# Two modulation vectors move from the first FFN to the first mixer, and the head's banks are emptied into two large buffers

## The chip, the cores and the metric

The kernel runs on one core of one Trainium2 chip. The metric is the device time of that core in microseconds (us). TensorE does the matmuls and the transposes; VectorE, ScalarE and GpSimd do the rest beside it; SyncE's queue issues the loads of the weights. Three runs of the kernel before gave 1095.24, 1098.37 and 1102.44 us, median 1098.37.

## The reference

A decoder trunk of two layers on 256 tokens of width 1024. Each layer is a half-step SwiGLU FFN (width 2816), a mixer with three groups of attention heads behind one input projection, and a second half-step FFN. Each of the three is modulated by nine vectors that come from one condition vector c.

```python
cond = jax.nn.silu(c)
for l in range(DEPTH):
    mod = cond @ ada_w[l] + ada_b[l]          # 1024 x 9216 weights in each layer
    (sh1, sc1, g1, sh2, sc2, g2, sh3, sc3, g3) = jnp.split(mod, N_MOD, axis=-1)
    n1 = modulate(rmsnorm(h, norm_ffn1[l]), sh1, sc1)
    h = h + MACARON_WEIGHT * g1[:, None, :] * swiglu(n1, ffn1_w_gu[l], ffn1_w_down[l])
    n2 = modulate(rmsnorm(h, norm_mix[l]), sh2, sc2)
    h = h + g2[:, None, :] * hybrid_mixer(n2, ...)
    n3 = modulate(rmsnorm(h, norm_ffn2[l]), sh3, sc3)
    h = h + MACARON_WEIGHT * g3[:, None, :] * swiglu(n3, ffn2_w_gu[l], ffn2_w_down[l])
```

The change concerns when sh3 and sc3 of layer 0 are computed: at any time before that layer's second FFN will do.

## The kernel before

**Weights.** All weights are float32 and come in the order of use, mostly as tiles `raw` of 128x2048 (1 MB), of which three exist; `load` (L217) issues each on SyncE's queue. `split` (L235) makes of each half tile a rounded copy `hi` (ScalarE, L243) and the remainder `lo` (VectorE, L244), both 128x1024, and TensorE multiplies hi by hi, hi by lo and lo by hi (L196). So every megabyte of a matmul weight costs VectorE two subtractions and ScalarE two copies.

**Modulation vectors.** A vector's weight is four tiles of 1 MB. `Ada.step` loads one of them and adds its two halves, each times a per-partition value of cond, into `acc` (VectorE, L433 for a vector's first half, L435 for the others): eight VectorE operations in all, and no work for TensorE until `finish`. There a gate (G1, G2, G3) takes a split of `acc`, four matmuls and two copies of ScalarE; a shift or scale (SH, SC) takes eight transposes, two reductions (L460) and one or two small operations. There is one buffer `acc`. ADA_PLAN says which vectors are computed in which sublayer, and `Jobs` spreads their steps, four for each vector, evenly over a number of places: over seven in the first FFN (JOB_PARTS), and in the mixer over the letters j of STEPS.

**Head.** The first FFN has eleven blocks of 256 columns. `lead` computes the first four of them while SC1 and SH1 of layer 0 are still being summed; it uses all eight banks of PSUM (four from psB, four from psA). At its end each bank is emptied by `row_act`: Silu on ScalarE, a multiplication on VectorE (L644), and the product `pr` is transposed back by TensorE (L201) into another bank and copied as a pair chh/chl (L709, L710). Blocks 4 to 10 follow: for each the two halves f of gate and up (`gu_mm`, matmuls into pb, 64 per block), the activation `gu_act` (L717 to L723, with GpSimd), and the products with the down weights (`down`, matmuls into pa, 24 per block) at the places that FIRST_DOWN gives.

**Mixer.** Its work is written as a list of letters in STEPS: M, a, b, q, c, V and p, w are projections that each need weights; h, b and C are heads with their softmax; i and r are the indexer and the eight rounds of the top-k, m the mask that comes of them; v and V are value projections; j is a place of `Jobs`. The scheduler of the tile framework takes the list as the order of emission, with a priority for some parts, and fixes each engine's order when the kernel is built; each engine then works through its own list in order.

Of the kernel before, what the change touches and what calls it, by code (L numbers as in the profile page):

```python
# [10 lines left out]
F32 = mybir.dt.float32  # L11
# [30 lines left out]
FIRST_DOWN = {4: [0, 1], 5: [2], 6: [3, 4], 7: [5], 8: [6, 7], 9: [8, 9], 10: [10]}  # L42
STEPS = [['a0', 'M0', 'M1', 'q1', 'q2', 'i0', 'q4', 'q3', 'q0', 'b1', 'i2', 'b3', 'a1', 'b0', 'j0', 'i4', 'b4', 'a2', 'i6', 'v0', 'r0', 'b2', 'r1', 'v1', 'h2', 'c0', 'c1', 'j1', 'c2', 'r2', 'c3', 'h0', 'j2', 'h4', 'r3', 'r4', 'j3', 'V0', 'V1', 'r5', 'c4', 'r6', 'j4', 'r7', 'm0', 'j5', 'p2', 'j6', 'z0', 'C0', 'p0', 'w0', 'p1', 'w2', 'w1', 'j7', 'p3', 'w3', 'C4', 'p4', 'C2', 'w4'], ['M0', 'M1', 'q4', 'q2', 'q0', 'q1', 'a0', 'i0', 'i2', 'q3', 'b1', 'a1', 'b0', 'i4', 'a2', 'b4', 'i6', 'b3', 'v0', 'r0', 'j0', 'v1', 'b2', 'h0', 'r1', 'c0', 'r2', 'c1', 'h2', 'c2', 'j1', 'j2', 'j3', 'r3', 'c3', 'h4', 'j4', 'j5', 'r4', 'r5', 'r6', 'r7', 'c4', 'V0', 'V1', 'm0', 'C2', 'z0', 'p0', 'p1', 'C0', 'j6', 'p2', 'C4', 'w0', 'p3', 'w2', 'j7', 'p4', 'w3', 'w4', 'w1']]
RS = 0
# [16 lines left out]
NEB = 3  # L61
ADA_PLAN = 'G1.SC2.SH2.SC3.SH3,G2,G3.1SC1.1SH1.1SC2,1SH2.1G1.1SC3.1SH3,1G2,1G3'
NEG = -1e30
# [124 lines left out]
def trunk(ctx, tc, stream, x, cols, rows, positions, rel_bias, ada_b, final_norm, onehot, addc, inv, crow, out, order):  # L188
# [423 lines left out]
    def ffn(l, wgu, wdn, nT, norm_fns, jobs, gate_v, first=False, tail=None):  # L612
# [3 lines left out]
        def get_gu(b):  # L616
            if b not in gu_units_:
                if b and (IO == 2 or IO == 1 and b == 1):
                    r = [load(gu_unit(wgu, l, b, side)) for side in range(2)]
                    w = [split(r[i % 2][:, i // 2 * 1024:(i // 2 + 1) * 1024]) for i in range(4)]  # L620
                    gu_units_[b] = (w[0::2], w[1::2])
                else:
                    gu_units_[b] = tuple(split_unit(load(gu_unit(wgu, l, b, side)), 2048) for side in range(2))
            return gu_units_[b]
# [14 lines left out]

        def row_act(p):  # L640
            sil = three("neg", name=nm("sil"))[:, 0:T]
            S.activation(sil, p[:, 0:256], AF.Silu)
            pr = three("pe", name=nm("pr"))[:, 0:T]
            V.tensor_tensor(pr, sil, p[:, 256:512], op=ALU.mult)  # L644
            return pr

        def lead():
# [25 lines left out]
            for k in range(KD):  # L673
# [20 lines left out]
                if k + 1 < KD:  # L694
                    ws[k + 1] = split_unit(raws[k + 1][2], 2048)
            with tc.high_priority(offset=HP):
                for i in range(LEADB):
                    pr = [row_act(p) for p in banks[i]]
                    p = psB()
                    for f in range(2):  # L700
                        for t in range(NT):
                            PE.transpose(p[:, (2 * f + t) * P:(2 * f + t + 1) * P], pr[t][:, f * P:(f + 1) * P], ident)
                    for f in range(2):
                        if i == LEADB - 1:
                            ch = [wk.tile([P, T], F32R, tag="pT", name=nm("cht"), bufs=PTB) for _ in range(2)]
                        else:
                            ch = chunk_tile()
                        pf = p[:, f * T:(f + 1) * T]
                        S.copy(ch[0], pf)  # L709
                        V.tensor_sub(ch[1], pf, ch[0].bitcast(F32))  # L710
                        act[2 * i + f] = ch

# [28 lines left out]

        def block(b):
            for f in (2 * b, 2 * b + 1):
                p = [psB(), psB()]
                gu_mm(p, f, rows_act if f == 2 else None)
                with tc.high_priority(offset=HP):
                    prior[:] = gu_act(p, f)

        def load_dn(b):
# [12 lines left out]
        if first:  # L762
            lead()
            open_acc()
            for b in range(LEADB, NB):
                now = FIRST_DOWN[b]
                load_dn(now[0])
                get_gu(b)
                if now[0] < NB - SKEW:
                    down_block(now[0])  # L770
                block(b)
                for d in now[1:]:
                    load_dn(d)
# [57 lines left out]
    def mixer(l, nT, norm_fns, jobs):  # L831
# [323 lines left out]
        for s in STEPS[l]:  # L1155
            if s[0] == "w":
                while int(s[1]) not in oT:
                    tick()
            do[s[0]](int(s[1]))
            if s[0] in TICK:  # L1160
                tick()
# [27 lines left out]
    for l in range(DEPTH):  # L1189
        nT, fns = norm(l, SC1, SH1) if l else (pair_tile(), None)  # L1190
        ffn(l, "ffn1_w_gu", "ffn1_w_down", nT, fns, Jobs(plan[l, 1], JOB_PARTS[2 * l]), G1, l == 0)
        nT, fns = norm(l, SC2, SH2)
        mixer(l, nT, fns, Jobs(plan[l, 2], 8))
        nT, fns = norm(l, SC3, SH3)
# [68 lines left out]
```

## Time and profile before

| | |
|---|---|
| median of three runs | 1098.37 us (1095.24 to 1102.44) |
| the profiled execution | 1097.09 us, span 1095.2 us, so 1.9 us lie outside the span |
| TensorE busy in the span | 1049.6 us (96%) |
| VectorE busy | 819.8 us (75%) |
| ScalarE, GpSimd busy | 620.1 us (57%), 194.9 us (18%) |
| mean granted clock of TensorE | 0.991 |

The stages of layer 0, by the timeline of TensorE: `lead` to 64.5 us, the rest of the first FFN ("the head" below) to 234.26, the mixer from there, with the matmuls of its V values (V0, V1) from 323.37, and then the second FFN; after that layer 1. Busy time is a share of the span for each engine; "pb" and "pa" are the two groups of PSUM banks. The granted clock of a stretch is a share of full speed: 1.00 is 2.4 GHz, 0.50 is 1.2 GHz.

### The profile page before, as it was taken

The page shows a single profiled execution, that of the slowest core. Times are in us where ns is not written, and L with a number is a line of the kernel's source. Part 1 is how long each engine was busy: PE and PEld are TensorE (multiplying, and loading weights), DVE is VectorE, ACT ScalarE, POOL GpSimd, SP SyncE. Part 2 cuts the span into 40 slices and gives each one's busy share as a digit, 9 for nine tenths or more (in the row PEclk, how much of TensorE's full clock was granted, in tenths as well). Part 3 has the DMA queues.
Part 4 walks back from the last instruction along what each step waited for, and adds up shares of the span by engine and source line. Part 5 has one row for each costly group of instructions (what it writes and reads, how often), then busy time and mean ns, then how long its engine had stood idle before and what let it go on. Part 6 is the DMA issues. An engine that isn't in the chain of part 4 may idle for free.

```text
span 1095.2 us, 15506 instructions
## 1 busy us (share of the span) xinstructions
PE 1049.6 (96%) x5634; PEld 878.2 (80%) x5634; DVE 819.8 (75%) x1334; ACT 620.1 (57%) x1177; POOL 194.9 (18%) x211
## 2 busy tenths in 40 slices
PE   5999999789999999999999999999999999999997
PEld 3778877668887688888878888887788778888885
DVE  6987877886795787786889877886669757656563
ACT  5554534366666766455555555555676667555561
POOL 1002221122000022232311323131200001222231
PEclk9999999899999999999999999999999999999999
DMA  8978887865355188787848888783536516666541
GB/s 340 373 267 296 293 320 269 334 223 189 111 188 193 64 298 290 270 303 267 293 160 303 292 303 293 281 313 132 188 125 208 178 58 210 233 227 224 212 183 38
DMA packets 38988, 255.84 MB, mean 234 GB/s; under 512 B 4824, under 2 KB 5208, under 8 KB 11008
## 3 DMA queue, kind: packets, MB, share of 16 engines
q1 hardware_dynamic: 38160, 253.14, 63.4%
q0 software_dynamic: 752, 1.71, 0.4%
q8 instruction: 44, 0.72, 0.3%
q14 instruction: 32, 0.26, 0.1%
HBM read 253.76 MB, written 1.07 MB: 233 GB/s over the span
## 4 chain that ended last, share of the span: by engine, by line
PE 80%; issue 6%; DVE 4%; ACT 4%; DMA 3%; POOL 2%; SPq 0%; DVEq 0%; POOLq 0%; ACTq 0%
PE pb L196 41%; PE pa L196 36%; PE pb L201 3%; DMA raw<-in_stream_dram 2%; DVE lo L244 1%; ACT hi L243 1%; DVE up L657 1%; PE pa L201 1%; POOL pr L721 1%; DMA invt<-in_inv_dram 1%; DVE acc L435 1%; POOL chl L723 1%; DMA scr<-gtab 0%; ACT nT L533 0%; ACT z L533 0%
## 5 line engine op out<-in xcount | busy, mean ns | idle before, releaser
L244 DVE TENSOR_TENSOR lo<-raw,hi 128x1024 fp32r<-128x1024 f32 (+3 forms) x314 | 380.7, 1227 | 145.5 <-ACT hi L243 143.5
L243 ACT CAST hi<-raw 128x1024 fp32r<-128x1024 f32 (+3 forms) x314 | 317.7, 1034 | 200.7 <-PE pb L196 94.0
L196 PE MATMUL pb<-nT,hi 128*128 128x512 f32 x1184 | 420.1, 396 | 5.3 <-ACT hi L243 5.3
L196 PE MATMUL pb<-nT,lo 128*128 128x256 f32 x1184 | 333.1, 284 | 2.2 <-DVE lo L244 2.2
L196 PEld LDWEIGHTS pb<-nT,hi 128*128 128x128 f32 x1184 | 222.9, 189 | 56.5 <-ACT hi L243 6.8
L196 PEld LDWEIGHTS pb<-nT,lo 128*128 128x128 f32 x1184 | 224.0, 189 | 6.1 <-DVE lo L244 3.1
L435 DVE SCALAR_TENSOR_TENSOR acc<-raw,cond,acc 128x1024 f32<-128x1024 f32 x118 | 155.5, 1317 | 20.1 <-DMA raw<-in_stream_dram 18.0
L721 POOL TENSOR_TENSOR pr<-sil,pr 128x256 f32<-128x256 f32 x74 | 76.8, 1038 | 516.4 <-DVE pr L718 310.6
L196 PE MATMUL pa<-hi,chh 128*128 128x512 f32 x328 | 105.0, 396 | 0.0
L196 PE MATMUL pa<-lo,chh 128*128 128x512 f32 x328 | 104.6, 392 | 0.4 <-DVE lo L244 0.4
L196 PE MATMUL pa<-hi,chl 128*128 128x512 f32 x328 | 103.3, 393 | 0.0
L196 PE MATMUL pa<-hi,nT 128*128 128x512 f32 (+3 forms) x320 | 89.2, 368 | 2.5 <-ACT nT L561 1.6
L723 POOL TENSOR_TENSOR chl<-pr,chh 128x256 fp32r<-128x256 f32 x74 | 81.7, 1105 | 53.6 <-ACT chh L723 53.6
L196 PEld LDWEIGHTS pa<-lo,chh 128*128 128x128 f32 x328 | 61.6, 189 | 13.5 <-DVE lo L244 0.8
L196 PEld LDWEIGHTS pa<-hi,chl 128*128 128x128 f32 x328 | 61.5, 189 | 13.1 <-issue 0.3
L196 PEld LDWEIGHTS pa<-hi,chh 128*128 128x128 f32 x328 | 60.3, 189 | 13.9 <-ACT chh L723 0.9
L196 PEld LDWEIGHTS pa<-hi,nT 128*128 128x128 f32 x320 | 58.8, 188 | 12.4 <-ACT nT L561 2.2
L196 PE MATMUL pa<-nT,hi 128*128 128x256 f32 x352 | 67.2, 289 | 0.0
L723 ACT CAST chh<-pr 128x256 fp32r<-128x256 f32 x74 | 30.0, 406 | 50.0 <-POOL pr L721 49.6
L196 PE MATMUL pb<-hi,nT 128*128 128x512 f32 x160 | 49.7, 413 | 8.4 <-ACT hi L243 3.9
L196 PEld LDWEIGHTS pa<-nT,hi 128*128 128x128 f32 x352 | 54.7, 189 | 3.3 <-issue 3.1
L196 PE MATMUL pa<-lo,nT 128*128 128x512 f32 (+3 forms) x160 | 54.2, 367 | 0.0
(210 smaller groups left out, 1278.2 us busy)
## 6 DMA issues: line engine op xcount, KB each, us to landing
raw<-in_stream_dram SPq DMA_DIRECT2D x218, 1024.0 KB, 4.9
up<-in_stream_dram SPq DMA_DIRECT2D x16, 512.0 KB, 12.6
raw<-in_stream_dram SPq DMA_DIRECT2D x4, 976.0 KB, 4.7
raw<-in_stream_dram SPq DMA_DIRECT2D x4, 768.0 KB, 4.3
raw<-in_stream_dram SPq DMA_DIRECT2D x4, 640.0 KB, 4.0
brev<-scr POOLq DMA_DIRECT2D x3, 512.0 KB, 10.6
h<-in_x_dram SPq DMA_DIRECT2D x2, 512.0 KB, 4.1
raw<-in_stream_dram SPq DMA_DIRECT2D x2, 512.0 KB, 3.6
```

Of the source, the lines that this page charges most:

```text
L196: last_pe[0] = nc.tensor.matmul(*a, **k)
L201: last_pe[0] = nc.tensor.transpose(*a, **k)
L243: ia = S.copy(hi[:, :n], src)
L244: iv = V.tensor_sub(lo[:, :n], src, hi[:, :n].bitcast(F32))
L435: iv = V.scalar_tensor_tensor(self.acc, src, cond[:, k:k + 1], self.acc, op0=ALU.mult, op1=ALU.add)
L657: V.tensor_tensor_reduce(out=src, in0=src, in1=condb, op0=ALU.mult, op1=ALU.add, scale=scale, scalar=first, accum_out=dst)
L721: G.tensor_tensor(pr, sil, pr, op=ALU.mult)
L723: last = [S.copy(ch[0], pr), G.tensor_tensor(ch[1], pr, ch[0].bitcast(F32), op=ALU.subtract)]
```

## The change

ADA_PLAN moves SC3 and SH3 of layer 0 from the first FFN (which keeps G1, SC2 and SH2, twelve steps over the same seven places) to the mixer, ahead of G2. The mixer's list for layer 0 gets twelve letters j in place of eight; they stand between its start and `r7`, and each is one step, while before four of the eight did one. `Jobs` takes the number of places from the list. In the head all eight banks are first emptied into two tiles `prods` of 128x1024; the transposes become a function `lead_turn`, which is called for the four blocks after the first half (f = 8) of block 4, and the first down weights are loaded behind it. So the weights of block 4 are loaded ahead of those of the first down block, and are split in the order gate, up, gate, up by half tiles.

```diff
--- before.py
+++ after.py
@@ -40,7 +40,7 @@
 LEADB = 4
 JOB_PARTS = [7, 11, 10, 9]
 FIRST_DOWN = {4: [0, 1], 5: [2], 6: [3, 4], 7: [5], 8: [6, 7], 9: [8, 9], 10: [10]}
-STEPS = [['a0', 'M0', 'M1', 'q1', 'q2', 'i0', 'q4', 'q3', 'q0', 'b1', 'i2', 'b3', 'a1', 'b0', 'j0', 'i4', 'b4', 'a2', 'i6', 'v0', 'r0', 'b2', 'r1', 'v1', 'h2', 'c0', 'c1', 'j1', 'c2', 'r2', 'c3', 'h0', 'j2', 'h4', 'r3', 'r4', 'j3', 'V0', 'V1', 'r5', 'c4', 'r6', 'j4', 'r7', 'm0', 'j5', 'p2', 'j6', 'z0', 'C0', 'p0', 'w0', 'p1', 'w2', 'w1', 'j7', 'p3', 'w3', 'C4', 'p4', 'C2', 'w4'], [
...
+STEPS = [['a0', 'M0', 'M1', 'q1', 'q2', 'i0', 'j', 'q4', 'q3', 'q0', 'b1', 'j', 'i2', 'b3', 'a1', 'b0', 'j', 'i4', 'b4', 'a2', 'j', 'i6', 'v0', 'r0', 'j', 'b2', 'r1', 'j', 'v1', 'h2', 'j', 'c0', 'c1', 'j', 'c2', 'r2', 'j', 'c3', 'h0', 'j', 'h4', 'r3', 'j', 'r4', 'V0', 'V1', 'r5', 'c4', 'r6', 'j', 'r7', 'm0', 'p2', 'z0', 'C0', 'p0', 'w0', 'p1', 'w2', 'w1', 'p3', 'w3', 'C4', 'p4', 'C2', 'w4'], [
...
 RS = 0
 SG = 1
 PL = 1
@@ -59,7 +59,7 @@
 TICKS = ['abcvVhC', 'abcvVhCw']
 DN = 0
 NEB = 3
-ADA_PLAN = 'G1.SC2.SH2.SC3.SH3,G2,G3.1SC1.1SH1.1SC2,1SH2.1G1.1SC3.1SH3,1G2,1G3'
+ADA_PLAN = 'G1.SC2.SH2,SC3.SH3.G2,G3.1SC1.1SH1.1SC2,1SH2.1G1.1SC3.1SH3,1G2,1G3'
 NEG = -1e30
 TOPK = T // 4
 IDXH = 8
@@ -615,7 +615,7 @@
 
         def get_gu(b):
             if b not in gu_units_:
-                if b and (IO == 2 or IO == 1 and b == 1):
+                if first and b == LEADB:
                     r = [load(gu_unit(wgu, l, b, side)) for side in range(2)]
                     w = [split(r[i % 2][:, i // 2 * 1024:(i // 2 + 1) * 1024]) for i in range(4)]
                     gu_units_[b] = (w[0::2], w[1::2])
@@ -637,10 +637,11 @@
             passes(p, t, lambda k: (ws[k // 2], slice((k % 2) * 512, (k % 2 + 1) * 512)), nT, between)
             return row_act(p)
 
-        def row_act(p):
+        def row_act(p, pr=None):
             sil = three("neg", name=nm("sil"))[:, 0:T]
             S.activation(sil, p[:, 0:256], AF.Silu)
-            pr = three("pe", name=nm("pr"))[:, 0:T]
+            if pr is None:
+                pr = three("pe", name=nm("pr"))[:, 0:T]
             V.tensor_tensor(pr, sil, p[:, 256:512], op=ALU.mult)
             return pr
 
@@ -693,22 +694,32 @@
                                       start=(k == 0 and x + y == 0), stop=(k == KD - 1 and y == 1))
                 if k + 1 < KD:
                     ws[k + 1] = split_unit(raws[k + 1][2], 2048)
+            prods = [x4(nm("prods")) for _ in range(2)]
+            for f in range(2 * LEADB - 2):
+                act[f] = chunk_tile()
             with tc.high_priority(offset=HP):
                 for i in range(LEADB):
-                    pr = [row_act(p) for p in banks[i]]
-                    p = psB()
-                    for f in range(2):
-                        for t in range(NT):
-                            PE.transpose(p[:, (2 * f + t) * P:(2 * f + t + 1) * P], pr[t][:, f * P:(f + 1) * P], ident)
-                    for f in range(2):
-                        if i == LEADB - 1:
-                            ch = [wk.tile([P, T], F32R, tag="pT", name=nm("cht"), bufs=PTB) for _ in range(2)]
-                        else:
-                            ch = chunk_tile()
-                        pf = p[:, f * T:(f + 1) * T]
-                        S.copy(ch[0], pf)
-                        V.tensor_sub(ch[1], pf, ch[0].bitcast(F32))
-                        act[2 * i + f] = ch
+                    for t, p in enumerate(banks[i]):
+                        c = (i % 2 * NT + t) * T
+                        row_act(p, prods[i // 2][:, c:c + T])
+            return prods
+
+        def lead_turn(prods, i):
+            with tc.high_priority(offset=HP):
+                p = psB()
+                for f in range(2):
+                    for t in range(NT):
+                        c = (i % 2 * NT + t) * T + f * P
+                        PE.transpose(p[:, (2 * f + t) * P:(2 * f + t + 1) * P], prods[i // 2][:, c:c + P], ident)
+                for f in range(2):
+                    if i == LEADB - 1:
+                        ch = [wk.tile([P, T], F32R, tag="pT", name=nm("cht"), bufs=PTB) for _ in range(2)]
+                    else:
+                        ch = act[2 * i + f]
+                    pf = p[:, f * T:(f + 1) * T]
+                    S.copy(ch[0], pf)
+                    V.tensor_sub(ch[1], pf, ch[0].bitcast(F32))
+                    act[2 * i + f] = ch
 
         def gu_act(ps2, f):
             sil = three("neg", name=nm("sil"))[:, 0:T]
@@ -739,12 +750,14 @@
                     S.copy(act[f][0], p[:, 0:T])
                     V.tensor_sub(act[f][1], p[:, 0:T], act[f][0].bitcast(F32))
 
-        def block(b):
+        def block(b, between=None):
             for f in (2 * b, 2 * b + 1):
                 p = [psB(), psB()]
                 gu_mm(p, f, rows_act if f == 2 else None)
                 with tc.high_priority(offset=HP):
                     prior[:] = gu_act(p, f)
+                if between:
+                    between(f % 2)
 
         def load_dn(b):
             dn_units_[b] = split_unit(load(dn_unit(wdn, l, b)), 2048, b >= NB - 2)
@@ -760,15 +773,26 @@
                     down(f, t, range(2))
 
         if first:
-            lead()
+            prods = lead()
+            get_gu(LEADB)
             open_acc()
+
+            def between(i):
+                if i == 0:
+                    for j in range(LEADB):
+                        lead_turn(prods, j)
+                    load_dn(0)
+
+            block(LEADB, between)
             for b in range(LEADB, NB):
                 now = FIRST_DOWN[b]
-                load_dn(now[0])
-                get_gu(b)
+                if b > LEADB:
+                    load_dn(now[0])
+                    get_gu(b)
                 if now[0] < NB - SKEW:
                     down_block(now[0])
-                block(b)
+                if b > LEADB:
+                    block(b)
                 for d in now[1:]:
                     load_dn(d)
                     if d < NB - SKEW:
@@ -1156,7 +1180,7 @@
             if s[0] == "w":
                 while int(s[1]) not in oT:
                     tick()
-            do[s[0]](int(s[1]))
+            do[s[0]](int(s[1:] or 0))
             if s[0] in TICK:
                 tick()
         while pend:
@@ -1190,7 +1214,7 @@
         nT, fns = norm(l, SC1, SH1) if l else (pair_tile(), None)
         ffn(l, "ffn1_w_gu", "ffn1_w_down", nT, fns, Jobs(plan[l, 1], JOB_PARTS[2 * l]), G1, l == 0)
         nT, fns = norm(l, SC2, SH2)
-        mixer(l, nT, fns, Jobs(plan[l, 2], 8))
+        mixer(l, nT, fns, Jobs(plan[l, 2], sum(x[0] == 'j' for x in STEPS[l])))
         nT, fns = norm(l, SC3, SH3)
         ffn(l, "ffn2_w_gu", "ffn2_w_down", nT, fns, Jobs(plan[l, 3], JOB_PARTS[2 * l + 1]), G3, tail=load_final if l == DEPTH - 1 else None)
     for t in range(NT):
```

Three places show what moves. First TensorE at the end of `lead`. Before, the transposes of the products pr follow the last matmul of lead (into pa_183), and the first down matmuls (into pa_594) stand between them:

```order
L196 MATMUL pa_183<-lo_477,nT_107 128x512
L201 MATMUL pb_518<-ident,pr_512 128x128
L201 MATMUL pb_518<-ident,pr_516 128x128
...
L201 MATMUL pb_539<-ident,pr_533 128x128
L201 MATMUL pb_539<-ident,pr_537 128x128
...
L201 MATMUL pb_560<-ident,pr_554 128x128
L196 MATMUL pa_594<-hi_600,chh_523 128x512
L196 MATMUL pa_594<-lo_601,chh_523 128x512
L196 MATMUL pa_594<-hi_600,chl_524 128x512
L201 MATMUL pb_560<-ident,pr_558 128x128
```

After, pb_572 and pb_573 are the two banks of the first half of block 4, and the four groups of transposes, of the products in `prods`, stand in and behind its matmuls; pa_568 is the first down product:

```order
L196 MATMUL pb_573<-nT_107,lo_557 128x256
L201 MATMUL pb_618<-ident,prods_510 128x128 x4
L196 MATMUL pb_573<-nT_107,hi_556 128x512
...
L196 MATMUL pb_573<-nT_107,lo_557 128x256
L201 MATMUL pb_627<-ident,prods_510 128x128 x4
L201 MATMUL pb_636<-ident,prods_511 128x128 x4
L201 MATMUL pb_645<-ident,prods_511 128x128 x4
L196 MATMUL pa_568<-hi_660,chh_512 128x512
```

The first of the transposes stands in place of row 197 at row 219, behind 22 more matmuls, and the down products come behind all sixteen.

Second, VectorE at the start of the mixer, where each of the remainders `lo` frees a half tile of weights. Before (ta, tb and cc are the rotation of a part of the queries, rep a copy of it):

```order
L826 TENSOR_TENSOR ta_2107<-cc_2095,cosf 128x64
L827 TENSOR_TENSOR tb_2108<-cc_2095,sinf 128x2x16
L828 TENSOR_TENSOR tb_2108<-cc_2095,sinf 128x2x16
L829 TENSOR_TENSOR cc_2095<-ta_2107,tb_2108 128x2x32
L888 COPY rep_2113<-cc_2095 128x128
L244 TENSOR_TENSOR lo_2174<-raw_2171,hi_2173 128x1024
L244 TENSOR_TENSOR lo_2178<-raw_2171,hi_2177 128x1024
L244 TENSOR_TENSOR lo_2288<-raw_2285,hi_2287 128x1024
L244 TENSOR_TENSOR lo_2292<-raw_2285,hi_2291 128x1024
```

After, the first two accumulations of SC3 (acc_2337) stand ahead of the same splits:

```order
L433 TENSOR_SCALAR acc_2337<-raw_2338,cond 128x1024
L850 TENSOR_TENSOR ta_2038<-cc_2026,cosf 128x64
L851 TENSOR_TENSOR tb_2039<-cc_2026,sinf 128x2x16
L852 TENSOR_TENSOR tb_2039<-cc_2026,sinf 128x2x16
L435 SCALAR_TENSOR_TENSOR acc_2337<-raw_2338,cond,acc_2337 128x1024
L853 TENSOR_TENSOR cc_2026<-ta_2038,tb_2039 128x2x32
L244 TENSOR_TENSOR lo_2105<-raw_2102,hi_2104 128x1024
L244 TENSOR_TENSOR lo_2109<-raw_2102,hi_2108 128x1024
L912 COPY rep_2044<-cc_2026 128x128
L244 TENSOR_TENSOR lo_2219<-raw_2216,hi_2218 128x1024
L244 TENSOR_TENSOR lo_2223<-raw_2216,hi_2222 128x1024
```

Such accumulations, with their loads on SyncE's queue, then stand between the splits of all the projections up to the V values.

Third, VectorE at the end of the top-k. Before, the V weights' last remainder (lo_3057) stands ahead of the last rounds of the top-k and of the mask msk:

```order
L938 MAX m_635_3193<-work_2279 128x8 x2
L244 TENSOR_TENSOR lo_3057<-raw_3050,hi_3056 128x640
L939 MATCH_REPLACE work_2279<-m_635_3193,work_2279 128x128
L939 MATCH_REPLACE work_2279<-m_635_3193,work_2279 128x256
L435 SCALAR_TENSOR_TENSOR acc_2889<-raw_3204,cond,acc_2889 128x1024
L938 MAX m_636_3198<-work_2279 128x8 x2
L435 SCALAR_TENSOR_TENSOR acc_2889<-raw_3204,cond,acc_2889 128x1024
L939 MATCH_REPLACE work_2279<-m_636_3198,work_2279 128x128
L939 MATCH_REPLACE work_2279<-m_636_3198,work_2279 128x256
L244 TENSOR_TENSOR lo_3154<-raw_3151,hi_3153 128x1024
L942 TENSOR_SCALAR msk_2280<-work_2279 128x384
```

After, the mask stands ahead of the V weights' first remainder (lo_3041), and accumulations of G2 (acc_2934) between the remainders:

```order
L966 TENSOR_SCALAR msk_2211<-work_2210 128x384
L1064 RECIPROCAL sm_2975<-sm_2975 128x2
L1055 ISA neg_3014,sm_3015<-pb_2999,biasm 128x128
...
L244 TENSOR_TENSOR lo_3041<-raw_3038,hi_3040 128x640
L435 SCALAR_TENSOR_TENSOR acc_2934<-raw_3029,cond,acc_2934 128x1024
L244 TENSOR_TENSOR lo_3045<-raw_3038,hi_3044 128x640
L1070 TENSOR_SCALAR pe_2978<-pe_2978,sm_2975 128x256
L1064 RECIPROCAL sm_2985<-sm_2985 128x2
```

Here the four splits of the V weights moved from ahead of the last two rounds of the top-k to behind the mask and behind four more softmax pieces (ISA, negation and sum). From the end of the mixer on, the orders of all engines are the same as before.

## Rows read from the trace of the kernel before

**Rows 1.** Page, the chain that ended last: shares of the span by engine.

```profile
PE 80%; issue 6%; DVE 4%; ACT 4%; DMA 3%; POOL 2%; SPq 0%; DVEq 0%; POOLq 0%; ACTq 0%
```

**Rows 2.** Stretches: length, busy PE, PEld, DVE, ACT, POOL, PEclk, DMA share, GB/s.

```profile
64.50:233.60 169.10, 154.78 (x766) 127.86 (x765) 138.53 (x176) 78.80 (x132) 34.44 (x37) 0.95 0.79 289
...
233.60:321.20 87.60, 85.91 (x556) 72.93 (x555) 70.55 (x194) 57.56 (x141) 6.81 (x13) 1.00 0.46 160
...
300.00:325.00 25.00, 25.00 (x186) 22.43 (x185) 23.78 (x85) 16.07 (x41) 0.00 (x0) 1.00 0.57 198
400.00:550.00 150.00, 150.00 (x802) 129.19 (x801) 116.44 (x127) 80.32 (x130) 43.38 (x37) 1.00 0.80 290
25.00:50.00 25.00, 24.25 (x103) 19.03 (x103) 24.52 (x37) 13.82 (x20) 0.00 (x0) 1.00 1.00 404
```

**Rows 3.** TensorE's waits from 64 to 234 us: total, times, longest.

```profile
PE pb L196 <- ACT hi L243: 5.3, 3, 2.7
PE pb L201 <- DVE pr L644: 2.5, 1, 2.5
PE pa L196 <- POOL chl L723: 2.3, 3, 1.3
PE pb L196 <- DVE lo L244: 2.2, 2, 1.5
```

**Rows 4.** Shorter stretches, columns as in Rows 2.

```profile
150.00:233.60 83.60, 71.79 (x343) 57.98 (x342) 66.28 (x78) 39.17 (x63) 17.29 (x19) 0.92 0.78 291
...
205.00:210.00 5.00, 2.48 (x7) 1.78 (x8) 4.40 (x4) 2.40 (x3) 0.00 (x0) 0.50 0.84 308
...
270.00:275.00 5.00, 4.88 (x29) 3.00 (x28) 1.23 (x1) 2.78 (x7) 2.99 (x8) 1.00 0.50 198
```

**Rows 5.** TensorE's timeline: start, length, operation, [idle before <- releaser].

```profile
67.73 0.85 PE L201 MATMUL pb<-ident,pr 128*128 128x128 f32 x4 [2.51 <-DVE pr L644]
...
74.43 0.39 PE L196 MATMUL pb<-nT,hi 128*128 128x512 f32 x1
...
234.26 1.06 PE L201 MATMUL pb<-ident,z 128*128 128x128 f32 x8
```

**Rows 6.** The chain in layer 0's second FFN: start, length, what.

```profile
439.87 11.19 PE pb L196 x64
451.06 5.47 PE pa L196 x24
```

**Rows 7.** VectorE's groups from 64.5 to 233.6: count, busy us, mean ns, idle.

```profile
L435 DVE SCALAR_TENSOR_TENSOR acc<-raw,cond,acc 128x1024 f32<-128x1024 f32 x36 | 47.2, 1311 | 2.1 <-DMA raw<-in_stream_dram 1.7
...
L460 DVE TENSOR_REDUCE modc<-pb 128x4 f32<-128x512 f32 x8 | 5.2, 685 | 2.9 <-PE pb L201 2.8
...
L433 DVE TENSOR_SCALAR acc<-raw,cond 128x1024 f32<-128x1024 f32 x4 | 3.0, 744 | 0.0
```

**Rows 8.** VectorE's groups from 233.6 to 321.2, columns as in Rows 7.

```profile
L244 DVE TENSOR_TENSOR lo<-raw,hi 128x1024 fp32r<-128x1024 f32 x15 | 18.1, 1221 | 2.9 <-ACT hi L243 2.8
L435 DVE SCALAR_TENSOR_TENSOR acc<-raw,cond,acc 128x1024 f32<-128x1024 f32 x6 | 7.8, 1298 | 5.5 <-DMA raw<-in_stream_dram 5.4
L244 DVE TENSOR_TENSOR lo<-raw,hi 128x768 fp32r<-128x768 f32 x4 | 3.8, 959 | 5.0 <-ACT hi L243 5.0
...
L244 DVE TENSOR_TENSOR lo<-raw,hi 128x640 fp32r<-128x640 f32 x4 | 3.3, 814 | 0.0
...
L1031 DVE CUSTOM_DVE_ANT_0 neg<-pb,biasm 128x256 f32<-128x256 f32 x7 | 2.9, 420 | 0.0
```

**Rows 9.** VectorE's timeline in the mixer, columns as in Rows 5.

```profile
273.77 2.70 DVE L435 SCALAR_TENSOR_TENSOR acc<-raw,cond,acc 128x1024 f32<-128x1024 f32 x2 [5.07 <-DMA raw<-in_stream_dram]
...
320.85 0.36 DVE L942 TENSOR_SCALAR msk<-work 128x384 fp32r<-128x384 f32 x1
```

**Rows 10.** TensorE's timeline in the mixer, first V matmul and first with the mask.

```profile
323.37 0.41 PE L196 MATMUL pa<-hi,nT 128*128 128x320 f32 x1
...
337.50 0.44 PE L196 MATMUL pb<-msk,identr 128*128 128x128 f32 x2
```

More of the change, by code (lines that the diff above doesn't have):

```diff
@@ L42 @@
 FIRST_DOWN = {4: [0, 1], 5: [2], 6: [3, 4], 7: [5], 8: [6, 7], 9: [8, 9], 10: [10]}
-STEPS = [['a0', 'M0', 'M1', 'q1', 'q2', 'i0', 'q4', 'q3', 'q0', 'b1', 'i2', 'b3', 'a1', 'b0', 'j0', 'i4', 'b4', 'a2', 'i6', 'v0', 'r0', 'b2', 'r1', 'v1', 'h2', 'c0', 'c1', 'j1', 'c2', 'r2', 'c3', 'h0', 'j2', 'h4', 'r3', 'r4', 'j3', 'V0', 'V1', 'r5', 'c4', 'r6', 'j4', 'r7', 'm0', 'j5', 'p2', 'j6', 'z0', 'C0', 'p0', 'w0', 'p1', 'w2', 'w1', 'j7', 'p3', 'w3', 'C4', 'p4', 'C2', 'w4'], ['M0', 'M1', 'q4', 'q2', 'q0', 'q1', 'a0', 'i0', 'i2', 'q3', 'b1', 'a1', 'b0', 'i4', 'a2', 'b4', 'i6', 'b3', 'v0', 'r0', 'j0', 'v1', 'b2', 'h0', 'r1', 'c0', 'r2', 'c1', 'h2', 'c2', 'j1', 'j2', 'j3', 'r3', 'c3', 'h4', 'j4', 'j5', 'r4', 'r5', 'r6', 'r7', 'c4', 'V0', 'V1', 'm0', 'C2', 'z0', 'p0', 'p1', 'C0', 'j6', 'p2', 'C4', 'w0', 'p3', 'w2', 'j7', 'p4', 'w3', 'w4', 'w1']]
+STEPS = [['a0', 'M0', 'M1', 'q1', 'q2', 'i0', 'j', 'q4', 'q3', 'q0', 'b1', 'j', 'i2', 'b3', 'a1', 'b0', 'j', 'i4', 'b4', 'a2', 'j', 'i6', 'v0', 'r0', 'j', 'b2', 'r1', 'j', 'v1', 'h2', 'j', 'c0', 'c1', 'j', 'c2', 'r2', 'j', 'c3', 'h0', 'j', 'h4', 'r3', 'j', 'r4', 'V0', 'V1', 'r5', 'c4', 'r6', 'j', 'r7', 'm0', 'p2', 'z0', 'C0', 'p0', 'w0', 'p1', 'w2', 'w1', 'p3', 'w3', 'C4', 'p4', 'C2', 'w4'], ['M0', 'M1', 'q4', 'q2', 'q0', 'q1', 'a0', 'i0', 'i2', 'q3', 'b1', 'a1', 'b0', 'i4', 'a2', 'b4', 'i6', 'b3', 'v0', 'r0', 'j0', 'v1', 'b2', 'h0', 'r1', 'c0', 'r2', 'c1', 'h2', 'c2', 'j1', 'j2', 'j3', 'r3', 'c3', 'h4', 'j4', 'j5', 'r4', 'r5', 'r6', 'r7', 'c4', 'V0', 'V1', 'm0', 'C2', 'z0', 'p0', 'p1', 'C0', 'j6', 'p2', 'C4', 'w0', 'p3', 'w2', 'j7', 'p4', 'w3', 'w4', 'w1']]
 RS = 0
```

## The prediction, made before the changed kernel ran

> **What bounds the kernel.** I read the chain of waits first: 80% of the span is TensorE's own work [rows 1]. Time is won or lost only where TensorE stands still or runs below full clock, or where its work changes; here its matmuls stay the same. So I looked for such stretches with the windows [rows 2]. Before `lead` ends the change alters nothing. From 64.5 to 233.6 us TensorE is busy 154.78 of 169.10 us, at a mean granted clock of 0.95. In the mixer up to 321.2 it is busy 85.91 of 87.60 at 1.00, and VectorE only 70.55 (81%). The second FFN, with the same blocks as the head, shows no idle time at all: 150.00 of 150, with VectorE at 116.44 (78%) and the loads at 290 GB/s. The head runs VectorE at 138.53 of 169.10 (82%) and does lose time; it has five modulation vectors to sum where the second FFN has four.
>
> What the head loses, I worked out from blocks at full pace: 11.19 us for a block of gate and up, 5.47 for one of down [rows 6]. Seven and eleven of them are 78.3 + 60.2 = 138.5 us; the 16 transposes of lead's products, the four vectors' 32 and the gate's few matmuls come to about 7.2 at 1.06 for eight transposes [rows 5]. That is 145.7 us of work in the 169.8 from 64.5 to the mixer's first transpose at 234.26 [rows 5]: **24.1 us lost**. Of it 14.3 (169.10 - 154.78 [rows 2]) are idle and the rest is slow clock: from 205 to 210, behind idle time, the clock was 0.50, which is 1.2 GHz, and TensorE busy 2.48 of 5 [rows 4]. So a microsecond of idle here costs 24.1 / 14.3 = 1.7 us.
>
> Where it is lost: 2.51 of the idle time are one wait at lead's end, for a product pr that VectorE makes [rows 3, 5]; up to 74.43, where block 4 begins [rows 5], TensorE does 13 transposes and 18 down matmuls, some 5.8 us of work in 9.9, so 4.1 are lost there. The other 20.0 lie behind 150 us, where 83.60 - 71.79 = 11.8 are idle [rows 4], for a weight's hi or lo (7.5 in both) and for the down inputs [rows 3].
>
> **The change part by part.** (a) *Two vectors fewer in the head.* Eight loads of 1 MB go, and on VectorE 2 x 0.744 + 14 x 1.311 = 19.8 us of sums and 4 x 0.685 = 2.7 of reductions [rows 7], about 23 with the small ones. TensorE's 16 transposes (2.1 us) go to the mixer with them: no gain. VectorE is left with 115.5 us for some 154, 75%, under the 78% at which the second FFN has no wait; the loads come to (289 x 169.1 - 8390) / 154, about 263 GB/s, under its 290. If that holds everywhere, the 11.8 us of idle vanish. The bounds are 0 and 11.8 us left. I take 2, nearest to the row of the second FFN, since the head still has three vectors in seven lumps and its first split waits for ScalarE; 2 x 1.7 = 3.4 us lost.
>
> (b) *The emptying at lead's end.* The wait of 2.51 goes: TensorE has 22 matmuls of block 4 to do, 3.9 us at 11.19 / 64, before and among the first transposes. What is late next: the fourth group of transposes needs a bank of block 4's first half, and VectorE's addition that frees it stands behind a subtraction of 1.22 [rows 8]; I estimate 2.1 us of idle. Then the first down matmul needs its weight and input from ScalarE, behind block 4's own copies: another 1.3. 3.4 x 1.7 = 5.8 us, where 4.1 are lost now. Bounds: nothing, when both are ready, and 10, when VectorE also has an accumulation ahead. So this part alone costs 1.7 us.
>
> The head gains 24.1 - 3.4 - 5.8 = **15 us** (bounds 24 and 0).
>
> (c) *Twelve steps in the mixer.* All come before r7, with their 8.4 MB in the same queue as the weights. The memory has room: 160 GB/s now [rows 2], 14.0 MB; 22.4 MB in about 92 us are 243, under 290. TensorE's 2.1 us were counted as moved. VectorE is the question, since each of its sums stands in one list with the remainders lo that TensorE needs. The mixer's first matmul that all this precedes is that of the V weights. VectorE's work before it: 70.55 now, less 7.8 for six sums and 26.4 for all splits (one more of 1.2 beside those of [rows 8]), leaves 36.4. Add the splits that now stand ahead of it, 14 x 1.221 + 4 x 0.959 + 0.814 + 1.2 = 22.9 [rows 8]; the sums, 18 x 1.298 + 2 x 0.744 = 24.9 [rows 7, 8]; four reductions, 2.7; and some 3.5 of small ones and four softmax pieces that were behind it. That is **90.4 us**. TensorE reaches the V matmul 323.37 - 233.6 = 89.8 us after the start [rows 10], with the 2.1 of transposes and about 0.9 of another head 92.8. VectorE must be busy 97% of that time for no stall. It was 98% from 25 to 50 us and 95% from 300 to 325, with TensorE 25.00 of 25 busy there [rows 2]; over the mixer it is 81%, but there it has no more work. I take 95%, the row of the same kind of work: 95.2 us, 2.4 late. The V weights' next remainders have two sums of 1.30 between them where none were: I add 1.3. At 1.7, that is **6 us** lost (bounds 0, at 98%, and 35, at 81%).
>
> (d) *The mask* came at 320.85 and was wanted at 337.50 [rows 9, 10]: 16 us of cover, and it moves ahead of the V weights, so nothing. If it were more than 16 us late, everything behind it would be too. G2 is wanted only with the mixer's last output, behind all the heads. The second FFN's norm finds SC3 and SH3 done long before; nothing else of it changes.
>
> Sum: -15 + 6 = **-9 us** on the profiled execution's 1097.09, which is 1.28 under the median of the runs shown. On the median's scale 1098.37 - 9 = **1089**.
>
> **One rule against it.** At 273.77 VectorE stood 5.07 us for the load of a sum [rows 9], and TensorE was busy 4.88 of the 5 us from 270 to 275 [rows 4]: one such wait was covered. The Trainium skill (TensorE: Matmul & The Clock Gate, the section Architectural detail: the array is 16× 32×32, not 1× 128×128) says that ACT and DVE queues are strict FIFO, so a sum whose load is late holds every remainder queued behind it. The trace agrees in that VectorE did nothing else in those 5 us, not in a price for TensorE. By the rule the sum would be that of the rival D below, by the row of TensorE that of (c); both are worked out from rows alone.
>
> **The rivals.** *B: both halves better.* The head becomes like the second FFN (nothing left of 2 us idle), and VectorE keeps 97% in the mixer. -24.1 + 5.8 + 1, about -17: 1081. For it: the 78% row. Against: the list of the mixer is twice as dense with sums as any that the trace shows over 90 us. *C: the head is only half cured.* Idle time behind 150 us waits for hi of ScalarE too (5.3 of it [rows 3]), which is not overloaded, so the loads' arrival in the three raw buffers may be what is late. Then half of 20.0 stays, the head gains 10 - 1.7 = 8, and the mixer takes 6 to 10: -2 to +2, so 1096 to 1100. *D: slower.* VectorE's list in the mixer waits again and again for the loads of sums, as at 273.77, and its share stays near 81%. 90.4 / 0.805 = 112.3, which is 19.5 behind TensorE's 92.8, and with the 1.3, at 1.7, costs 35: -15 + 35 = +20, 1118. It decides from the share at which the loss equals the head's 15: 15 / 1.7 - 1.3 = 7.5 late, 90.4 / 100.3 = 90%. Against it: in the densest stretch, 300 to 325, VectorE had 95%, and at 81% it had nothing to do for part of the time. *That the change does nothing* is excluded by the order of the instructions.
>
> **The numbers.** 1% is 11 us, about what a measurement of this kernel can tell from no change; faster means under 1087.4, slower over 1109.4. The forecast (1084 to 1095) has 0.45, of which 0.17 is faster; B 0.22, all faster; C 0.21, all the same; D 0.12, of which 0.02 comes out the same at a share near 88%. Faster 0.17 + 0.22 = 0.39, with 0.01 of C's lucky end 0.40; slower 0.10 and 0.01 for a late mask, 0.11; same 0.49. The range from 1079 (B with a little more) to 1103 (C's upper end and a bit) leaves out D and the ends of B, some 0.15 to 0.2. B, the forecast and C have one sign or none; D alone the other.
>
> **What would show it.** Right: from 75 us to the mixer TensorE waits 4 us or less and at a clock of 1.00; the mixer's first transpose comes at about 219, not 234; at lead's end the 2.51 is gone and two waits of one to two us appear, for VectorE's sil and for ScalarE's chh; the first V matmul comes about 95 us behind the mixer's start, with a wait for lo of 2 to 4 us ahead. Wrong: waits for hi of over 6 us in the head (C), or a V matmul over 100 us behind the mixer's start with VectorE idle for raw (D).

## The result, and the profile after

The changed kernel took 1104.26 us (median of 14 runs, 1099.53 to 1112.75), the kernel before 1097.19 (14 runs). The ratio is 1.0071, 95% interval 1.0047 to 1.0096: **slower by 0.7%**, where 1089 was forecast and the range ended at 1103. The profiled execution has a span of 1104.3 us, 9.1 more than before.

The windows of the changed kernel, columns as in [rows 2], show the head in two pieces, then the mixer up to its first V matmul, the V matmuls themselves, and the whole mixer:

```profile
64.50:80.00 15.50, 11.57 (x56) 9.55 (x56) 12.11 (x20) 7.80 (x19) 2.35 (x2) 0.80 0.79 305
80.00:219.97 139.97, 136.82 (x694) 113.93 (x692) 105.38 (x134) 69.80 (x113) 36.46 (x33) 1.00 0.72 262
219.97:325.20 105.23, 93.81 (x589) 78.91 (x589) 85.68 (x220) 56.54 (x143) 13.35 (x15) 0.96 0.52 188
325.20:335.00 9.80, 8.01 (x32) 6.89 (x33) 8.76 (x22) 6.37 (x18) 0.00 (x0) 0.58 0.63 221
219.97:381.61 161.64, 147.16 (x858) 119.72 (x859) 122.88 (x299) 91.61 (x226) 15.78 (x18) 0.95 0.52 188
```

The same two stretches of the mixer before, up to the first V matmul and from there to the next norm:

```profile
234.26:323.37 89.11, 87.49 (x569) 74.39 (x570) 71.01 (x197) 58.74 (x143) 6.81 (x13) 1.00 0.47 166
323.37:373.38 50.01, 48.75 (x275) 38.12 (x274) 31.64 (x80) 32.86 (x84) 2.56 (x3) 1.00 0.40 147
```

TensorE's timeline of the changed kernel, columns as in [rows 5], has the two waits at lead's end, the mixer's first transpose, the first two V matmuls, and the next norm's transposes:

```profile
73.14 0.66 PE L201 MATMUL pb<-ident,prods 128*128 128x128 f32 x4 [2.10 <-DVE pr L729]
75.63 1.22 PE L196 MATMUL pa<-hi,chh 128*128 128x512 f32 x2 [1.83 <-ACT chh L720]
...
219.97 1.06 PE L201 MATMUL pb<-ident,z 128*128 128x128 f32 x8
...
325.20 0.63 PE L196 MATMUL pa<-hi,nT 128*128 128x320 f32 x1 [4.92 <-ACT hi L243]
327.27 0.63 PE L196 MATMUL pa<-lo,nT 128*128 128x320 f32 x1 [1.44 <-DVE lo L244]
...
381.61 1.06 PE L201 MATMUL pb<-ident,z 128*128 128x128 f32 x8 [0.46 <-DVE z L511]
```

Three differences add up. The mixer began 14.3 us earlier (219.97, before 234.26 [rows 5]). It lasted 161.64 us, before 139.12: 22.5 longer. Behind it another 0.9 were lost. -14.3 + 22.5 + 0.9 = 9.1. The head gained most of what was forecast, and the mixer gave it all back and more. Of the 22.5, 16.1 lie ahead of the first V matmul (105.23 against 89.11) and 6.4 behind it, where the clock granted in the V matmuls was 0.58 of full speed, near the level of 1.2 GHz. Over the whole mixer TensorE was idle 14.5 us (161.64 - 147.16), before 2.9, so 11.6 of the 22.5 are idle time. Another 2.1 are the 16 transposes that moved, and the remaining 8.8 are the mixer's own work at a lower clock: the granted clock was 0.95, before 1.00.

TensorE's waits of the changed kernel, in the head and then in the mixer (total, times, longest):

```profile
PE pb L201 <- DVE pr L729: 2.1, 1, 2.1
PE pa L196 <- ACT chh L720: 1.8, 1, 1.8
PE pa L196 <- ACT chh L734: 1.1, 2, 0.7
PE pb L196 <- DVE lo L244: 1.0, 1, 1.0
PE pb L196 <- ACT hi L243: 0.8, 1, 0.8
```

```profile
PE pa L196 <- ACT hi L243: 4.9, 1, 4.9
PE pa L201 <- ACT pe L1068: 2.6, 1, 2.6
PE pb L201 <- POOL iqq L853: 1.8, 1, 1.8
PE pa L196 <- DVE lo L244: 1.8, 2, 1.4
```

The head's waits for hi and lo fell from 7.5 us [rows 3] to 1.8. In the mixer there are four new lines of over 1.5 us, where no line was over 0.8 us before; one of three such lines of before is:

```profile
PE pa L196 <- ACT nT L561: 0.8, 1, 0.8
```

**The longest of them, followed back.** The chain of waits of the changed kernel around the V matmuls (start, length, what):

```profile
312.01 0.97 POOL acc L426
312.98 0.28 issue
313.26 2.54 DMA acc<-in_ada_b_dram
315.81 0.26 DVE work L963
316.07 1.09 issue
317.16 1.29 DVE acc L435
318.44 0.40 DVE work L963 x2
318.84 0.07 DVE chl L1103
318.91 0.18 issue
319.09 1.28 DVE acc L435
320.37 0.03 DVE m L962
320.39 4.01 DMA raw<-in_stream_dram
```

The last row is the load of the V weights. It could be issued only at 320.39, when a sum of G2 (319.09) had freed a raw tile. That sum had waited for the memset of the one buffer acc (312.01) and the load of G2's bias into it (313.26), and the memset for SH3's transposes. So the V weights, which need nothing of G2, were late by way of the shared raw tiles and the one acc. The delay of the sums began earlier, as VectorE's and TensorE's timelines show:

```profile
258.16 1.37 DVE L435 SCALAR_TENSOR_TENSOR acc<-raw,cond,acc 128x1024 f32<-128x1024 f32 x1
...
286.44 0.42 DVE L1103 TENSOR_TENSOR chl<-pb,chh 128x256 fp32r<-128x256 f32 x1 [5.03 <-ACT chh L1103]
286.78 1.28 DVE L460 TENSOR_REDUCE modc<-pb 128x4 f32<-128x512 f32 x2
287.98 0.74 DVE L433 TENSOR_SCALAR acc<-raw,cond 128x1024 f32<-128x1024 f32 x1
```

```profile
285.92 1.09 PE L201 MATMUL pb<-ident,acc 128*128 128x128 f32 x8
```

SC3's last sum was done by 259.5, but its transposes stand at 285.92 in TensorE's list, so SH3's first sum came at 287.98. In between VectorE stood waiting for TensorE's and ScalarE's results; it was idle for 19.6 us (105.23 - 85.68) in the mixer up to the V matmul, and its longest waits there were:

```profile
DVE work L956 <- ACT rel L953: 6.0, 3, 3.8
DVE chl L1103 <- ACT chh L1103: 5.0, 1, 5.0
DVE lo L244 <- ACT hi L243: 2.8, 2, 1.9
...
DVE acc L433 <- DMA raw<-in_stream_dram: 0.6, 1, 0.6
```

For a sum's load it waited 0.6 us, not 5.07 at a time as at 273.77 before [rows 9]. In this stretch the sums hardly waited for loads, and the one load followed here, that of the V weights, waited for a sum.

### The profile page after: what moved, and what is told of

It reads as the page before. It is cut to its first block, busy times and chain, and to the rows that moved or that the text cites. A ratio compares the mean times of both kernels' runs of the same rounds, so it can differ in the third digit from the quotient of the medians.

```text
span 1104.3 us, 15493 instructions
## 1 busy us (share of the span) xinstructions
PE 1054.6 (96%) x5634; PEld 881.2 (80%) x5634; DVE 819.0 (74%) x1334; ACT 616.9 (56%) x1177; POOL 207.6 (19%) x211
## 4 chain that ended last, share of the span: by engine, by line
PE 76%; issue 7%; DMA 5%; DVE 5%; ACT 4%; POOL 2%; SPq 0%; DVEq 0%; POOLq 0%; ACTq 0%
PE pb L196 40%; PE pa L196 34%; DMA raw<-in_stream_dram 4%; PE pb L201 2%; DVE lo L244 2%; ACT hi L243 1%; DVE up L658 1%; DVE acc L435 1%; DMA invt<-in_inv_dram 1%; POOL pr L732 1%; PE pa L201 0%; ACT z L533 0%; POOL chl L734 0%; ACT nT L533 0%; ACT nT L561 0%
## 5 line engine op out<-in xcount | busy, mean ns | idle before, releaser
L732 POOL TENSOR_TENSOR pr<-sil,pr 128x256 f32<-128x256 f32 x74 | 84.8, 1146 | 498.5 <-DVE pr L729 374.7
L196 PEld LDWEIGHTS pa<-lo,chh 128*128 128x128 f32 x328 | 61.9, 189 | 13.1
```

Of the source, the lines that this page charges most:

```text
L196: last_pe[0] = nc.tensor.matmul(*a, **k)
L732: G.tensor_tensor(pr, sil, pr, op=ALU.mult)
```

## The experiments

Two theories were set first. Theory L: the V weights' load is held in the raw tiles, as the chain shows. Theory W: VectorE has too much work ahead of the V weights. "Head" below is the time of the mixer's first transpose, "mixer" the time from it to the next norm's.

**One part alone.** The kernel before with the new ADA_PLAN and the new list of STEPS, and the changed kernel with the old ones:

```diff
-ADA_PLAN = 'G1.SC2.SH2.SC3.SH3,G2,...'
+ADA_PLAN = 'G1.SC2.SH2,SC3.SH3.G2,...'
-        mixer(l, nT, fns, Jobs(plan[l, 2], 8))
+        mixer(l, nT, fns, Jobs(plan[l, 2], sum(x[0] == "j" for x in STEPS[l])))
```

> Only the move of SC3 and SH3 to the mixer with its twelve places; lead's end is the old one. Theory L (loads held: in the mixer the three raw buffers hold tiles whose sums VectorE's list puts late, so the V weights' load is issued late): the mixer's first transpose at 216 to 219 us (15 to 18 earlier than 234.26), the mixer about 22 us longer than before, the V matmuls again behind a wait for hi of 4 to 6 us; 1099 to 1104 us. Theory W (VectorE has too much work ahead of the V weights): the same times. Rival E (the emptying at lead's end is what costs): as fast as the head's gain, 1080 to 1084 us.

> Only the rewrite of lead's end; plan and places are the old ones. Theories L and W: 1098 to 1102 us, 1 to 4 us more than before, all of it between 64 and 85 us (two waits of about 2 us and half clock behind them). Rival E: 1104 us or more.

The plan alone: 1105.00 us, ratio 1.0058 (1.0043 to 1.0073), head 215.98, mixer 166.2. Lead's end alone: 1098.20, ratio 0.9997 (0.9986 to 1.0008), head 236.03 (1.8 later than before), mixer 139.1. So rival E falls: the moved vectors make the loss, and lead's new end costs nothing that can be told from its runs' times. The plan alone began the mixer 4.0 us earlier than the changed kernel, but its mixer lasted 4.5 longer, and the medians of the two kernels are 0.7 apart, within their spread.

**The V weights' load set free.** The twelve loads go to pairs of large tiles instead of raw tiles:

```diff
-            raw = load(ada_unit(l, v, i))
+            raw = load_halves(ada_unit(l, v, i)) if (l, v) in OWN else load(ada_unit(l, v, i))
```

> The changed kernel, but the twelve loads for SC3, SH3 and G2 of the first mixer go to pairs of 128x1024 tiles of the pool of large buffers instead of raw tiles; same bytes, same sums. Theory L: the V weights' load is no longer behind a sum; first V matmul 92 to 96 us behind the mixer's first transpose (105.2 in the changed kernel) with a wait of at most 1 us; 1086 to 1092 us. Theory W: VectorE still has the same 25 us of sums among the splits; the V matmul 102 us or later behind the start, or the same stall at another place of the mixer; 1099 to 1104 us.

1116.39 us, ratio 1.0156 (1.0133 to 1.0179). The wait at the V matmul was gone and it came 101.4 us behind the start, but the mixer lasted 172.1 us, with these waits of TensorE ahead:

```profile
PE pa L201 <- ACT pe L1079: 11.6, 6, 4.4
PE pa L201 <- DVE pe L1081: 3.8, 3, 2.3
```

The stall moved to the softmax pieces. **Theory L as the whole cause falls**, with a reserve: the edit also moved the sums in VectorE's list, and in this order VectorE did wait for the sums' loads, by its waits in the mixer:

```profile
DVE acc L446 <- DMA ada<-in_stream_dram: 7.0, 7, 1.8
DVE acc L444 <- DMA ada<-in_stream_dram: 6.9, 1, 6.9
```

**Half of the sums left out.** The loads stay, of each only the first half is summed:

```diff
-            for kk in range(2):
+            for kk in range(1 if (l, v) in ((0, SC3), (0, SH3), (0, G2)) else 2):
```

> The changed kernel with the second half of each of the twelve loads not summed (left out: half of SC3, SH3 and G2's sums); loads, transposes and places stay. Theory W: about 13 us less for VectorE ahead of the V weights; no wait there, the first V matmul 93 us behind the mixer's first transpose; 1087 to 1091 us. Theory L: SH3's first sum still waits for SC3's transposes (at 286 in the changed kernel) and the V weights' load still for a sum that stands behind the top-k; only the sums left out behind 287 us (8 x 1.3 = 10 us of VectorE) come off, the V matmul 97 to 101 us behind the start, still with a wait of 2 us or more; 1094 to 1099 us.

1094.10 us, ratio 0.9965 (0.9949 to 0.9980); no wait for hi, V matmul 94.6 us behind the start, but mixer 150.1. The V matmul is near theory W's place, the total is theory L's: with 13.5 us less of VectorE's work the mixer was 11.6 shorter, and it was still 11 longer than before. (With fewer sums the scheduler also built a somewhat different order for VectorE.)

**Other places.** A new theory P: only the places were wrong. The places of the twelve steps were moved; the list shows the letters behind which a j stands (SC3, SH3, G2):

```
early:          a0 M1 i0 q0 | b1 i2 b3 b0 | v1 c0 c2 c3
G2 late:        i0 b1 b0 a2 | r0 r1 h2 c1 | r6 m0 p2 w1
early, G2 late: a0 M1 i0 q0 | b1 b3 b0 b4 | r6 m0 p2 w1
SC3 only:       i0 b1 b0 a2 |             | r6 m0 p2 w1   (SH3 stays in the first FFN)
```

> The changed kernel with its twelve places earlier: SC3's four behind a0, M1, i0, q0, SH3's behind b1, i2, b3, b0, G2's behind v1, c0, c2, c3; loads, sums and transposes are the same, all twelve still ahead of the V weights. Theory P (the places, not the sum of the work: in the changed kernel VectorE stands idle for 20 us from 259 to 287 because SC3's transposes, and with them the one buffer of the sums and the raw tiles, come 27 us behind its last sum, and is full from 287 to 326): SC3's transposes come by 265 us, VectorE is idle for under 10 us from 255 to 290, the first V matmul 95 to 98 us behind the mixer's first transpose (105.2 in the changed kernel), 1088 to 1093 us. Theory W (VectorE has too much work ahead of the V weights, wherever it stands): V matmul 102 us behind or later, 1099 to 1106 us.

> The changed kernel with G2's four places moved behind the V weights (r6, m0, p2, w1); SC3 and SH3 stay where they are. Theory W: 9 us of sums less ahead of the V weights, V matmul 94 to 96 us behind the mixer's first transpose, and VectorE has room behind it: 1088 to 1092 us. Theory P: the V load is free of G2's sums, but SH3's still bunch behind SC3's late transposes: V matmul 96 to 99 us behind, the waits near 300 us stay; 1092 to 1097 us.

> SC3's and SH3's places early (behind a0, M1, i0, q0, b1, b3, b0, b4) and G2's behind the V weights. Theories P and W: no wait over 1.5 us in the mixer, V matmul 92 to 94 us behind its first transpose, the head's 14 us kept but for the 2 us of transposes: 1083 to 1088 us. If it is not under 1090, neither the places nor the work ahead of the V weights is what holds the mixer.

> SH3 stays in the first FFN (sixteen steps over seven places); only SC3 goes to the mixer, at the first four of the changed kernel's places, G2 behind the V weights as in the run before. Theory W: mixer 141 to 143 us long; the head keeps part of its loss (mixer's first transpose at 224 to 230): 1088 to 1095 us. Theory P says the same of the mixer; it is a measure of the head with four vectors.

Early: 1100.92 us, ratio 1.0035 (1.0017 to 1.0052). SC3's transposes came at 259.84 and VectorE was busier ahead of the V weights than in any other run with twelve steps there, and still the V matmul came 106.7 us behind the start: **theory P falls** on its main number, and both of theory W's hold (102 us or later, 1099 to 1106). Its window up to the V matmul:

```profile
218.04:324.78 106.74, 93.57 (x581) 78.85 (x581) 92.67 (x217) 58.61 (x143) 10.26 (x17) 0.94 0.62 226
```

G2 late: 1097.77, ratio 1.0007 (0.9994 to 1.0020), V matmul 98.9 behind, mixer 153.2 (the profiled execution, 1094.11, was the shortest of the ten). Taking G2's four steps from ahead of the V weights took away the wait for hi and 6.3 us ahead of them. The run does not part the price of the chain shown above from that of G2's sums, since both left that stretch. The V matmul is where theory P had it; the total missed both expectations, theory P's by 0.8.

Early and G2 late: 1094.29, ratio 0.9965 (0.9947 to 0.9983), faster than both kernels, but over the 1090 set as a bound: its V matmul came 97.9 us behind, its mixer lasted 151.0. By that bound neither the places nor the work ahead of the V weights is the whole of it. Its windows, to the V matmul and from there:

```profile
219.23:317.12 97.89, 91.79 (x585) 77.55 (x586) 86.86 (x217) 57.39 (x143) 8.81 (x15) 0.98 0.59 212
317.12:370.21 53.09, 50.22 (x274) 39.21 (x274) 35.04 (x83) 33.32 (x84) 2.45 (x3) 0.97 0.51 185
```

SC3 only: 1104.81, ratio 1.0061 (1.0046 to 1.0076). Expected were a head of 224 to 230 and a mixer of 141 to 143; measured 233.29 and 146.2. By the reckoning of the prediction a head with four vectors loses 168.8 - 144.6 = 24.2 us. With the same new end of lead, one with five loses 171.5 - 145.7 = 25.8 (from the run with lead's end alone), and one with three 11.9. Nearly the whole gain of the head comes with the second vector.

**Work and loads by themselves.** Two new theories, V (VectorE's time) and R (the loads). First the sums cut to 32 of 1024 columns (all but SC3's and SH3's first) with all loads kept; then the sums kept with three loads instead of twelve, in the kernel with own tiles, where the order of VectorE and TensorE stays the same:

```diff
+                    n = 32 if (l, v) in ((0, SC3), (0, SH3), (0, G2)) else D
-                    iv = V.scalar_tensor_tensor(self.acc, src, cond[:, k:k + 1], self.acc, op0=ALU.mult, op1=ALU.add)
+                    iv = V.scalar_tensor_tensor(self.acc[:, :n], src[:, :n], cond[:, k:k + 1], self.acc[:, :n], op0=ALU.mult, op1=ALU.add)
...
+            elif i == 0:
+                self.halves = raw = load_halves(ada_unit(l, v, i))
+            else:
+                raw = self.halves
```

> The changed kernel with its twelve loads, places, transposes and number of operations, but each sum but a vector's first reads and writes only 32 of 1024 columns (left out: most of SC3, SH3 and G2's sums). VectorE's work in the mixer falls below that of the kernel before. Theory V (what the mixer pays for is VectorE's time, since each sum stands in one list with the remainders and the softmax pieces that TensorE waits for): mixer 140 to 143 us long (139.1 before, 161.6 in the changed kernel), nearly all of it the 2 us of transposes; 1082 to 1087 us. Theory R (it is the loads, which share three raw tiles and one queue with the weights): mixer 146 us or longer; 1089 us or more.

> The kernel with own tiles for the sums' loads, with only the first load of each of the three vectors: all 24 sums are done, those of steps 2 to 4 on the tiles of step 1 (left out: nine of the twelve loads, so SC3, SH3 and G2 are sums of the wrong rows). Order of all engines as in the run with own tiles. Theory V: mixer within 4 us of that run's 172.1 us. Theory R: 155 us or shorter.

Loads without sums: 1092.87 us, ratio 0.9972 (0.9946 to 0.9999); mixer 147.2, as theory R had it, in these two pieces:

```profile
218.87:312.45 93.58, 91.04 (x589) 76.70 (x589) 67.71 (x217) 55.21 (x139) 9.26 (x15) 1.00 0.60 220
312.45:366.10 53.65, 50.52 (x270) 38.55 (x270) 33.33 (x83) 35.75 (x88) 2.43 (x3) 1.00 0.51 185
```

Sums with few loads: 1105.16, ratio 1.0075 (1.0046 to 1.0103), mixer 160.7 where the run with the loads had 172.1, between the two theories. **Neither theory alone holds.** Against the changed kernel 161.6 - 147.2 = 14.4 of the 22.5 us went with the sums; of the 8.1 left, 2.1 are the 16 transposes that moved, and 6.0 come with the loads and the rest of the new order. Two things blur the 14.4: with the shorter sums the scheduler also built another order for VectorE and TensorE, above all from the top-k on, so part of it may be the order's, and the medians of the two kernels differ by only 11.4. In the order with own tiles, which is the same in both runs, nine loads carry 11.4. Those loads hold no raw tile. VectorE's wait for the sums' loads fell there from 13.9 us to this:

```profile
DVE acc L451 <- DMA ada<-in_stream_dram: 6.8, 1, 6.8
```

These shares belong to one order each.

**Toward a better kernel.** The early places with G2 late and lead's old end; and the same with SH3's places at b0, a2, r1, c1:

> SC3 and SH3 early and G2 behind the V weights, as in the run of 1094.3, but with lead's old end, which began the mixer 4 us earlier than the new one where the rest was the same (215.98 to 219.97): 1089 to 1092 us, faster than before by 0.5 to 0.8%. If lead's end made no difference, 1093 to 1096.

> As the run before, but SH3's four places wider apart (b0, a2, r1, c1 instead of b1, b3, b0, b4). Theory V: the stretch in which VectorE was full and TensorE waited (262 to 284 us) is thinner, but the same work comes ahead of the V weights: mixer 147 to 152 us, 1087 to 1092 us.

The first: 1092.28 us, ratio 0.9953 (0.9934 to 0.9973), the lowest median of all that compute the whole; head 218.72, mixer 152.7. The 4 us expected of lead's old end don't show in its head, but the profiled execution was the longest of its ten (1096.49), so this says little; by the medians it is 2.0 us faster than with the new end, and the two intervals overlap. The second: 1097.91, ratio 1.0005 (0.9985 to 1.0025), mixer 158.1 where 147 to 152 was expected; spreading SH3 made it worse.

## Why the prediction was wrong

**Right: the head.** The lost time in it was 24.1 us; now it is 155.5 (from 64.5 to 219.97) less 143.6 of work (145.7 less 2.1), so 11.9. The gain is 12.2, where 15 was forecast. The first transpose came at 219.97 and was forecast at about 219, but that nearness is partly luck: by the prediction's own terms it was 234.26 - 15 - 2.1 = 217, since the moved transposes leave the head too. Behind 80 us it is idle 139.97 - 136.82 = 3.2 us at a clock of 1.00; 2 was taken. At lead's end both forecast waits are there, 2.10 (2.1 forecast) and 1.83 (1.3); the first releaser is the second of VectorE's two additions, not the first, and the loss there is near 8.7 us (11.9 - 3.2) rather than 5.8. The single parts say the same. With the plan alone the head lost 151.5 - 143.6 = 7.9, so part (a) gained 16.2, where 20.0 - 3.4 = 16.6 was forecast. Part (b), priced at 1.7, cost 1.8 in the head with five vectors and 4.0 in the head with three, from one profiled execution each.

**Wrong: step (c), the twelve steps in the mixer.** It was priced at 6 us (bounds 0 and 35). The mixer became 22.5 longer, 20.4 without the transposes. Of the 18.1 us between the forecast -9 and the measured 9.1, 14.4 (20.4 - 6) are this step's; 2.8 are the head's, and 0.9 came behind the mixer. The step took a share of 95% for VectorE up to the V matmul, from the row of 25 us at 300 to 325 [rows 2]. Measured are 85.68 of 105.23, 81%: the share of before (71.01 of 89.11 is 80%). The work ahead was sized about right (85.7, forecast 90.4); the share was not. In no run with eight or twelve steps ahead was it above 89%, however the steps were placed (92.67 of 106.74 and 86.86 of 97.89 are the highest). A row of 25 us in which VectorE nearly always had something ready said nothing of 100 us in which it waits in turn for TensorE and ScalarE, as its waits above show. That "there it has no more work" was the reason to set the 81% aside, and it was wrong: with more work the share stayed at 81% in this order, and rose to 89% at most in others.

**Rival D** had that share, with 12% chance. Its mechanism was not the one of this kernel: it let VectorE wait for the sums' loads, which took 0.6 us; the chain shows a load of weights waiting for a sum. (In the order with own tiles the wait that it meant is there, 13.9 us.) The rule it leaned on (the Trainium skill, TensorE: Matmul & The Clock Gate, the section Architectural detail: the array is 16× 32×32, not 1× 128×128: ACT and DVE are strict FIFO) agrees with the trace: VectorE stood idle for 1.09 us from 316.07 ahead of the sum at 317.16, and the top-k's step at 318.44 came only behind that sum. Its price (+20) was too high: the V matmul came 12.4 us behind the forecast 92.8 instead of 19.5, since VectorE's work ahead of it was 85.7 us and not 90.4. The rate of 1.7 held: 20.4 us were lost for 11.6 more of idle time, 1.76 for each. (The forecast counts from 233.6, 0.7 us ahead of the mixer's first transpose, and the 105.23 are counted from that transpose; so the lateness on one scale is 13.1.)

**Also missed in (c):** the loads. They were priced at nothing since the memory had room (188 GB/s measured ahead of the V matmul, under 290). But the run with hardly any sums still had a mixer 6.0 us longer, and nine loads made 11.4 in the order with own tiles, so "nothing" was wrong. By what way loads cost is not shown: in the changed kernel the chain runs through the three raw tiles, but the nine loads that cost 11.4 stood in tiles of their own. The prediction also missed that one buffer acc ties each vector to the last one's transposes, which came 26 us behind SC3's last sum; that this tie cost time is not shown, as the V matmul was no earlier with these transposes at 259.84.

**Rival C** missed its place (behind 80 us the head waited only 0.8 us for hi), and B fell with the share.

## What to carry to other kernels

From this case: the idle share of an engine that works through its list in order is not room for more work. See what share it ever reached over a stretch as long as the one you fill, and price the added work at that share. When loads move, look at the buffers that they will hold and at who frees them, not only at the bandwidth. Work moved between stages in one piece should be priced stage by stage: in seven kernels with the same twelve steps in raw tiles, the head gave 14 to 20 us, and the mixer took 12 to 27. An edit that takes work out can also change the order that the scheduler builds, so compare the orders before the difference is put down to the work.

## What was not expected of the hardware

A head with four vectors lost nearly as much as one with five, 24.2 us and 25.8, with VectorE at 130.95 of 168.79 us, 78%, the share at which the second FFN lost nothing [rows 2]. So a share of 78% does not by itself mean that nothing is lost; why the fourth vector costs so much is not shown. Behind the wait of 4.92 us the V matmuls ran at a granted clock of 0.58 for 9.8 us.
